# The first group's residual adds in a tiled matmul with bias and residual: from six in a row on GpSimd to four on VectorE, one a tile, and four on GpSimd

## The chip, the cores and the metric

The kernel runs on one core of a Trainium2 chip. The metric is the device time of one execution in microseconds, the median of several runs. A core has five engines with instruction streams of their own: TensorE (PE in the profile; its weight loads are PEld), VectorE (DVE), ScalarE (ACT), GpSimd (POOL) and SyncE (SP), which in this kernel only issues DMAs. Each engine executes its own instructions in order, and semaphores tie the engines together.

## The reference

```python
batch, m, k, n = 16, 512, 1024, 768        # x, weight, bias, residual: float32
def reference(x, weight, bias, residual):
    return (np.matmul(x, weight) + bias + residual).astype(np.float32)
```

Flattened, x is 8192 x 1024, weight 1024 x 768, residual and output 8192 x 768.

## The kernel before

**Tiles and groups.** The 8192 rows are 64 tiles (`n_sub`) of 128 rows. Eight tiles (`G` = 8) form a group, so there are eight groups. A group's x is one load of 4 MB (`load_x`), its residual one load of 3 MB (`load_r`) and its output one store of 3 MB (`store`), but for the first x group, which comes in pieces, and the last store, which goes in pieces. All are issued by SP through one queue, in the order of the program.

**A tile's way.** ScalarE casts the tile's x to bf16 (`cast_x`, L120), three tiles ahead. TensorE transposes it in eight pieces into PSUM (`transpose`, L135, tile `pt`, two buffers). VectorE copies that to SBUF (`copy_xt`, L142, tile `xt`, four buffers). TensorE multiplies it with the weights, which stay in SBUF, in sixteen matmuls (`matmul`, L149, tile `po`, three buffers). VectorE takes the result out of PSUM (`evacuate`).

**What is added where.** For groups 1 to 7 the eviction adds the product to the residual in place (L166), and GpSimd then adds the bias to the same tile, SBUF to SBUF (`add_bias`, L173). Group 0 is different: its residual is not there yet when its tiles are multiplied, so its eviction adds the bias (L163) and writes to a tile of its own, `o_tile`. The residual is added later, SBUF to SBUF, by `add_residual` (L177), eight such adds for the group's eight tiles. Its second argument names the engine; GpSimd is the default.

**The loop** over t (L263 to L286) holds for each tile, in this order: cast of tile t + 3; transposes of tile t + 1, then the matmuls of tile t, on TensorE; copy of tile t + 1 and eviction of tile t on VectorE; and the DMAs that `moves` (L243) lists for this t. The order of each engine's instructions is that of the program, kept by the wrapper `o(...)`. In the kernel before, the residual adds 0 and 1 are on VectorE in tiles 16 and 17, between the copy and the eviction (L277, L278), and 2 to 7 are on GpSimd at the end of tile 15 (L282 to L284), behind the bias add of tile 15 and ahead of that of tile 16.

**Buffers.** Four homes of 3 MB (the ring) hold the residuals and outputs of the groups; `HOME` gives the home of each group: r0 and r3 share home 3, r1 and r4 home 1, r2 and r6 home 0; `o_tile` of group 0 and r5 share home 2. So the load of r3 (listed at t = 17) waits for all eight residual adds, which read r0, that of r4 (t = 21) for the store of group 1, and that of r5 (t = 29) for the store of group 0. Behind the load of r0 and r2 (t = 5), SP's queue goes on with x3 (t = 12), store 1 (t = 15), r3 (t = 17), x4 (t = 20), r4 and store 0 (t = 21), x5 (t = 28), r5 and store 2 (t = 29).

Of the kernel before, what the change touches and what calls it, by code (L numbers as in the profile page):

```python
# [11 lines left out]
G = 8  # L12
# [9 lines left out]
def kernel(  # L22
# [8 lines left out]
    nc = tc.nc  # L31
# [27 lines left out]
    def o(ins):  # L59
        return tc.keep_in_program_order(ins)  # L60
# [49 lines left out]
    def cast_x(t, split=False):  # L110
        if t >= n_sub:
            return
        xb_tiles[t] = slot(xb_pool, "xb", XB_BUFS, [P, K], BF16)
        src = x_tiles[t // G][:, t % G, :]
        if split:
            h = K // 2
            o(nc.scalar.copy(out=xb_tiles[t][:, :h], in_=src[:, :h]))  # L117
            o(nc.vector.tensor_copy(out=xb_tiles[t][:, h:], in_=src[:, h:]))  # L118
        else:
            o(nc.scalar.copy(out=xb_tiles[t], in_=src))  # L120
# [7 lines left out]
    def transpose(t):  # L128
        if t >= n_sub:
            return  # L130
        xb = xb_tiles.pop(t).rearrange("m (h p j) -> m h j p", p=P, j=4)
        pt = slot(pt_pool, "pt", PT_BUFS, [P, n_k, P], BF16)
        for k in range(n_k):
            h, j = divmod(k, 4)
            o(nc.tensor.transpose(out=pt[:, k, :], in_=xb[:, h, j, :], identity=ident))  # L135
        pt_tiles[t] = pt

    def copy_xt(t):
        if t >= n_sub:
            return  # L140
        xt_tiles[t] = slot(xt_pool, "xt", XT_BUFS, [P, n_k, P], BF16)
        o(nc.vector.tensor_copy(out=xt_tiles[t], in_=pt_tiles.pop(t)))  # L142

    def matmul(t, k0=0, k1=n_k):
        if t not in po_tiles:
            po_tiles[t] = slot(po_pool, "po", PO_BUFS, [P, N], FP32)
        for k in range(k0, k1):
            for (n0, nl) in chunks:
                o(nc.tensor.matmul(  # L149
                    po_tiles[t][:, n0:n0 + nl],  # L150
                    lhsT=xt_tiles[t][:, k, :],
                    rhs=w_sb[:, k, n0:n0 + nl],
                    start=(k == 0),
                    stop=(k == n_k - 1),
                ))

    def evacuate(t):


        g, j = divmod(t, G)  # L160
        po = po_tiles.pop(t)
        if g == 0:
            o(nc.vector.tensor_add(out=o_tiles[0][:, j, :], in0=po, in1=bias_bc))  # L163
        else:
            rt = r_tiles[g][:, j, :]
            o(nc.vector.tensor_add(out=rt, in0=po, in1=rt))  # L166
            if t < n_sub - 3:
                add_bias(t)
        xt_tiles.pop(t)

    def add_bias(t, engine=nc.gpsimd):
        rt = r_tiles[t // G][:, t % G, :]
        o(engine.tensor_add(out=rt, in0=rt, in1=bias_bc))  # L173

    def add_residual(t, engine=nc.gpsimd):
        ot = o_tiles[0][:, t, :]
        o(engine.tensor_add(out=ot, in0=ot, in1=r_tiles[0][:, t, :]))  # L177
# [85 lines left out]
    for t in range(3, n_sub - 1):  # L263
        cast_x(t + 3)
        if t == 3:
            matmul(t, 0, 5)
            transpose(t + 1)
            matmul(t, 5, 8)
        elif t == G - 1:
            matmul(t, 0, 2)  # L270
            transpose(t + 1)
            matmul(t, 2, 8)
        else:
            transpose(t + 1)
            matmul(t)
        copy_xt(t + 1)
        if t in (2 * G, 2 * G + 1):  # L277
            add_residual(t - 2 * G, nc.vector)  # L278
        evacuate(t)
        if t in (n_sub - 9, n_sub - 7, n_sub - 5):  # L280
            add_bias(n_sub - 3 + (t - n_sub + 9) // 2)
        if t == 2 * G - 1:  # L282
            for u in range(2, G):
                add_residual(u)  # L284
        for move, *what in moves.get(t, []):
            move(*what)  # L286


    t = n_sub - 1
# [36 lines left out]
```

## Time and profile before

| | us |
|---|---|
| median of 3 runs | 211.21 (211.03 to 211.63) |
| the profiled execution, its time | 210.92 |
| the profiled execution, its span | 209.1 |
| TensorE busy in the span | 199.5 (95%) |
| VectorE busy | 107.3 (51%) |
| ScalarE busy | 67.7 (32%) |
| GpSimd busy | 114.4 (55%) |
| DMA, 87.28 MB | mean 417 GB/s |

The span goes from the first to the last instruction of the profiled execution; its time, as the runs are timed, has 1.8 us more around it. The granted TensorE clock is at full speed throughout. The instructions in question, from the page's groups (count, busy us in total, mean ns of one):

| | engine | count | busy us | mean ns |
|---|---|---|---|---|
| matmuls L149 | TensorE | 978 | 172.1 | 324 |
| copies L142 | VectorE | 64 | 43.6 | 682 |
| evictions L166 | VectorE | 55 | 52.7 | 958 |
| residual adds L177 | VectorE | 2 | 3.3 | 1647 |
| residual adds L177 | GpSimd | 6 | 12.1 | 2056 |
| bias adds L173 | GpSimd | 56 | 101.0 | 1814 |

The matmuls are pipelined, so their durations overlap. Busy shares are averages over the whole span; idle time of an engine that others do not wait for costs nothing.

### The profile page before, as it was taken

How to read it: one execution, taken by the hardware profiler on the slowest of the kernel's cores; microseconds unless marked ns; L12 is line 12 of the kernel's file. 1: busy time of each engine (PE TensorE's matmuls, PEld its weight loads, DVE VectorE, ACT ScalarE, POOL GpSimd, SP SyncE). 2: the span in 40 equal slices, each digit the busy share in tenths (PEclk: the TensorE clock that was granted, in tenths of full speed). 3: DMA queues.
4: the chain of work that ended last, by engine and by line, in shares of the span. 5: the costliest groups of instructions: out<-in, count | busy, mean ns of one | idle time of the engine just before them, and what ended most of it. 6: DMA issues, size and time to landing. Idle time of an engine off the chain costs nothing.

```text
span 209.1 us, 3593 instructions
## 1 busy us (share of the span) xinstructions
PE 199.5 (95%) x1520; PEld 130.8 (63%) x1550; DVE 107.3 (51%) x142; ACT 67.7 (32%) x70; POOL 114.4 (55%) x69
## 2 busy tenths in 40 slices
PE   7679999999999999999999999999999999999992
PEld 2346766666666666666666666666666666666661
DVE  0457555455478545454554554455445445544542
ACT  2446309507331074303632063310733018320000
POOL 2000000365579999966556655655665565599820
PEclk9999999999999999999999999999999999999999
DMA  6999999999999999999999999999999999999994
GB/s 241 416 424 445 461 418 412 464 400 437 431 453 396 418 439 395 454 445 414 431 431 445 418 414 451 434 426 429 417 432 431 461 409 423 417 434 442 409 385 192
DMA packets 5066, 87.28 MB, mean 417 GB/s; under 512 B 565, under 2 KB 694, under 8 KB 1594
## 3 DMA queue, kind: packets, MB, share of 16 engines
q1 hardware_dynamic: 5040, 87.03, 97.8%
q8 instruction: 12, 0.20, 0.4%
q14 instruction: 4, 0.03, 0.0%
q10 hardware_dynamic: 10, 0.01, 0.0%
HBM read 61.88 MB, written 25.17 MB: 416 GB/s over the span
## 4 chain that ended last, share of the span: by engine, by line
PE 82%; DMA 14%; ACT 1%; issue 1%; SPq 0%; DVE 0%; ACTq 0%
PE po L149 69%; PE pt L135 12%; DMA x_tile<-in_x_dram 11%; DMA bias_rows<-in_bias_dram 2%; PE last_ps L293 1%; ACT L76 1%; ACT xb L120 1%; SPq L91 0%; DVE r_tile L296 0%; ACT warm L76 0%; ACTq L120 0%; ACTq L184 0%
## 5 line engine op out<-in xcount | busy, mean ns | idle before, releaser
L149 PE MATMUL po<-w_sb,xt 128*128 128x256 bf16 (+1 forms) x978 | 172.1, 324 | 2.6 <-DVE xt L142 0.8
L173 POOL TENSOR_TENSOR r_tile<-r_tile,bias_bc 128x768 f32<-128x768 f32 x56 | 101.0, 1814 | 85.2 <-DVE r_tile L166 85.2
L149 PEld LDWEIGHTS <-xt 128*128 128x128 bf16 x1008 | 95.8, 98 | 58.9 <-DVE xt L142 1.4
L120 ACT CAST xb<-x_tile 128x1024 bf16<-128x1024 f32 x61 | 61.2, 1044 | 108.5 <-DMA x_tile<-in_x_dram 64.6
L166 DVE TENSOR_TENSOR r_tile<-po,r_tile 128x768 f32<-128x768 f32 x55 | 52.7, 958 | 79.1 <-PE po L149 73.2
L142 DVE COPY xt<-pt 128x1024 bf16<-128x1024 bf16 x64 | 43.6, 682 | 3.1 <-PE pt L135 3.1
L135 PEld LDWEIGHTS <-xb 128*128 128x128 bf16 x512 | 35.4, 113 | 11.0 <-ACT xb L117 3.0
L135 PE MATMUL pt<-ident,xb 128*128 128x128 bf16 x512 | 39.1, 219 | 2.2 <-ACT xb L117 2.2
L177 POOL TENSOR_TENSOR o_tile<-o_tile,r_tile 128x768 f32<-128x768 f32 x6 | 12.1, 2056 | 0.0
L163 DVE TENSOR_TENSOR o_tile<-po,bias_bc 128x768 f32<-128x768 f32 x8 | 7.6, 955 | 7.0 <-PE po L149 7.0
L199 PE MATMUL warm_ps<-warm_in 128*128 128x512 bf16 x14 | 5.3, 530 | 1.0 <-DVE warm L75 1.0
L124 ACT CAST w_sb<-w_stage 128x768 bf16<-128x768 f32 x4 | 3.3, 832 | 3.7 <-DMA w_stage<-in_weight_dram 3.7
L118 DVE CAST xb<-x_tile 128x512 bf16<-128x512 f32 x3 | 1.3, 424 | 6.0 <-DMA x_tile<-in_x_dram 6.0
L199 PEld LDWEIGHTS <-warm_in 128*128 128x128 bf16 x14 | 1.7, 131 | 3.4 <-issue 2.4
L117 ACT CAST xb<-x_tile 128x512 bf16<-128x512 f32 x3 | 1.8, 615 | 5.6 <-DMA x_tile<-in_x_dram 5.6
L177 DVE TENSOR_TENSOR o_tile<-o_tile,r_tile 128x768 f32<-128x768 f32 x2 | 3.3, 1647 | 0.0
L126 DVE CAST w_sb<-w_stage 128x768 bf16<-128x768 f32 x4 | 2.2, 556 | 1.7 <-DMA w_stage<-in_weight_dram 1.7
L293 PE MATMUL last_ps<-w_sb,xt 128*128 128x512 bf16 (+1 forms) x16 | 2.8, 326 | 0.0
L293 PEld LDWEIGHTS <-xt 128*128 128x128 bf16 x16 | 1.6, 98 | 1.1
L296 DVE TENSOR_TENSOR r_tile<-last_ps,r_tile 128x512 f32<-128x512 f32 (+1 forms) x2 | 1.1, 558 | 0.9 <-PE last_ps L293 0.8
L76 ACT ACT_TABLE_LOAD x1 | 1.3, 1283 | 0.7 <-PEq L310 0.7
L227 DVE STREAM_SHUFFLE bias_bc<-bias_rows 128x768 f32<-128x768 f32 x1 | 1.0, 1006 | 0.0
(11 smaller groups left out, 2.1 us busy)
## 6 DMA issues: line engine op xcount, KB each, us to landing
x_tile<-in_x_dram SPq DMA_DIRECT2D x7, 4096.0 KB, 29.2
r_tile<-in_residual_dram SPq DMA_DIRECT2D x8, 3072.0 KB, 17.7
out_dram<-r_tile SPq DMA_DIRECT2D x6, 3072.0 KB, 23.9
x_tile<-in_x_dram SPq DMA_DIRECT2D x4, 1024.0 KB, 8.8
w_stage<-in_weight_dram SPq DMA_DIRECT2D x4, 768.0 KB, 6.5
out_dram<-o_tile SPq DMA_DIRECT2D x1, 3072.0 KB, 31.2
out_dram<-r_tile SPq DMA_DIRECT2D x1, 1536.0 KB
out_dram<-r_tile SPq DMA_DIRECT2D x1, 768.0 KB, 5.5
```

Of the source, the lines that this page charges most:

```text
L76: o(nc.scalar.copy(out=warm, in_=warm))
L120: o(nc.scalar.copy(out=xb_tiles[t], in_=src))
L124: o(nc.scalar.copy(out=w_sb[:, k, :], in_=w_stage[0][:, k, :]))
L135: o(nc.tensor.transpose(out=pt[:, k, :], in_=xb[:, h, j, :], identity=ident))
L142: o(nc.vector.tensor_copy(out=xt_tiles[t], in_=pt_tiles.pop(t)))
L149: o(nc.tensor.matmul(po_tiles[t][:, n0:n0 + nl], lhsT=xt_tiles[t][:, k, :], rhs=w_sb[:, k, n0:n0 + nl], start=(k == 0), stop=(k == n_k - 1),))
L163: o(nc.vector.tensor_add(out=o_tiles[0][:, j, :], in0=po, in1=bias_bc))
L166: o(nc.vector.tensor_add(out=rt, in0=po, in1=rt))
L173: o(engine.tensor_add(out=rt, in0=rt, in1=bias_bc))
L177: o(engine.tensor_add(out=ot, in0=ot, in1=r_tiles[0][:, t, :]))
L199: o(nc.tensor.matmul(warm_ps, lhsT=warm_in, rhs=warm_in[:, None, :].to_broadcast([P, 4, P]), start=True, stop=True))
L293: o(nc.tensor.matmul(ps, lhsT=xt_tiles[t][:, k, :], rhs=w_sb[:, k, n0:n0 + nl], start=(k == 0), stop=(k == n_k - 1)))
```

## The change

VectorE takes four residual adds, 0 to 3, in tiles 14 to 17, each behind the eviction of its tile and not in front of it. GpSimd takes the other four: add 7 in tile 14, between the bias adds of tiles 14 and 15, and 6, 5, 4 at the end of tile 15. VectorE's stream thus gets two adds more (tiles 14 and 15), and in tiles 16 and 17 the order add, eviction becomes eviction, add; GpSimd's loses two. No DMA is added or taken out, and the order of SP's queue is the same.

```diff
         copy_xt(t + 1)
-        if t in (2 * G, 2 * G + 1):
-            add_residual(t - 2 * G, nc.vector)
         evacuate(t)
+        if 2 * G - 2 <= t < 2 * G + 2:
+            add_residual(t - 2 * G + 2, nc.vector)
         if t in (n_sub - 9, n_sub - 7, n_sub - 5):
             add_bias(n_sub - 3 + (t - n_sub + 9) // 2)
-        if t == 2 * G - 1:
-            for u in range(2, G):
+        if t == 2 * G - 2:
+            add_residual(G - 1)
+        elif t == 2 * G - 1:
+            for u in range(G - 2, 3, -1):
                 add_residual(u)
         for move, *what in moves.get(t, []):
             move(*what)
```

## The prediction

> **What bounds the kernel now.** I read the page's chain of waits first, then the waits of TensorE alone, then the timelines of VectorE, GpSimd and TensorE around tiles 14 to 19, and last the busy shares at the very end.
>
> ```profile
> PE 82%; DMA 14%; ACT 1%; issue 1%; SPq 0%; DVE 0%; ACTq 0%
> q1 hardware_dynamic: 5040, 87.03, 97.8%
> ```
>
> The first line is the chain that ended last: 82% of it is TensorE, and the 14% of DMA lies at the start (one piece from 8.09 to 31.50 us, the load of x group 1). From 31.6 us to 205.5 us it names TensorE alone, with 0.05 us of issue every two tiles or so. The second line is the DMA queue, which is almost as full. So two resources run side by side, and the question is which one the end follows.
>
> ```profile
> PE pt L135 <- ACT xb L117: 2.2, 2, 1.1
> PE warm_ps L199 <- DVE warm L75: 1.0, 1, 1.0
> PE po L149 <- DVE xt L142: 0.8, 1, 0.8
> PE po L149 <- ACT w_sb L124: 0.3, 1, 0.3
> ```
>
> These are all the waits of TensorE (us in total, times, longest). By their lines they belong to the start (L117, L75, L124; the 0.8 is at 12.56 us). In the steady loop TensorE never waits, and a tile takes 3.05 us.
>
> ```profile
> 204.00:205.00 1.00, 1.00 (x9) 0.71 (x8) 0.32 (x1) 0.00 (x0) 0.00 (x0) 1.00 0.48 197
> 205.00:206.00 1.00, 0.45 (x5) 0.16 (x2) 0.80 (x2) 0.00 (x0) 0.00 (x0) 1.00 0.83 335
> ```
>
> The last two figures of a row are the DMA share and GB/s. In the last us of matmuls the DMA engines are half idle (0.48): the queue has run dry and the last stores wait for TensorE. So TensorE sets the end: whatever delays it in the loop comes out at the end, and a gain can come only from it.
>
> **The resource that the change touches.** In the timeline of VectorE and GpSimd, the first two figures are start and duration in us.
>
> ```profile
> 60.73 1.81 POOL L173 TENSOR_TENSOR r_tile<-r_tile,bias_bc 128x768 f32<-128x768 f32 x1 [1.24 <-DVE r_tile L166]
> 61.16 2.19 DVE L177 TENSOR_TENSOR o_tile<-o_tile,r_tile 128x768 f32<-128x768 f32 x1
> 62.50 2.53 POOL L177 TENSOR_TENSOR o_tile<-o_tile,r_tile 128x768 f32<-128x768 f32 x1
> 63.28 0.94 DVE L166 TENSOR_TENSOR r_tile<-po,r_tile 128x768 f32<-128x768 f32 x1
> 64.14 0.68 DVE L142 COPY xt<-pt 128x1024 bf16<-128x1024 bf16 x1
> 64.74 1.10 DVE L177 TENSOR_TENSOR o_tile<-o_tile,r_tile 128x768 f32<-128x768 f32 x1
> 65.79 0.96 DVE L166 TENSOR_TENSOR r_tile<-po,r_tile 128x768 f32<-128x768 f32 x1
> ```
>
> The same residual add on VectorE takes 2.19 or 1.10 us, and on GpSimd 2.53 where others take 1.81. The ends explain it. GpSimd's bias add ends at 60.73 + 1.81 = 62.54; VectorE's add, begun at 61.16, ends at 63.35, 0.81 later. GpSimd's next ends at 62.50 + 2.53 = 65.03, 1.68 after VectorE's end. VectorE's second add ends at 65.84, again 0.81 after GpSimd's 65.03. So the two take turns whole instruction by whole instruction: VectorE's add waits for GpSimd's running one to end and then needs 0.81; GpSimd's next then needs 1.68 from there. Evictions (0.96) and copies (0.68) keep their durations, so only the adds with both inputs in SBUF take part.
>
> The cover for a long VectorE add is the slack of the copy behind it, which the timeline of TensorE gives:
>
> ```profile
> 59.49 0.61 PE L135 MATMUL pt<-ident,xb 128*128 128x128 bf16 x8
> 59.94 2.76 PE L149 MATMUL po<-w_sb,xt 128*128 128x512 bf16 x16
> 62.54 0.61 PE L135 MATMUL pt<-ident,xb 128*128 128x128 bf16 x8
> ```
>
> Matmuls of tile 16 start at 59.94, of 17 at 62.99, of 18 at 66.03, of 19 at 69.08, and each needs its copied tile (L142) about 0.05 us before: in the one such wait the copy ended at 11.82 + 0.69 = 12.51 and the matmul began at 12.56.
>
> **The change, step by step.** It takes two adds (1.81 each) off GpSimd, which nobody on the chain waits for, and puts VectorE's adds in tiles 14 to 17, behind the eviction and thus in front of the copy that TensorE needs next. Before, VectorE's two stood in front of the eviction of 16 and 17, whose lateness three PSUM buffers hid. GpSimd's order becomes bias 14, add 7, bias 15, adds 6, 5, 4, bias 16.
>
> An add that meets nobody isn't in the trace. Its bounds are 0.81 (the time after a wait) and 1.10 (the shortest row, wait included); the eviction with as many elements takes 0.96. I take 0.88. An instruction on VectorE starts 0.08 before the one ahead ends, on GpSimd 0.04.
>
> Tile 14: eviction 56.65 to 57.61; add 0 from 57.53 to 58.41; GpSimd's bias add, released by the same eviction at 57.68, finds VectorE first and ends at 58.41 + 1.68 = 60.08 instead of 59.49. Copy 16 ends at 59.01, in time. Tile 15: add 7 on GpSimd from 60.04 to 61.85; VectorE evicts until 60.65 and begins add 1 at 60.57, into it: it ends at 61.85 + 0.81 = 62.67. Copy 17 behind it ends at 63.27, where the matmul was due at 62.99: it begins at 63.33, **0.34 us late**. Tile 16: the eviction ends at 64.15; add 2, begun at 64.07, meets bias 15 (held by add 1, ending 64.35) and ends at 65.16; copy 18 ends at 65.76, due 66.37: in time. Tile 17: add 6, held by add 2, ends at 66.84; add 5 begins at 66.80; VectorE's eviction, late with TensorE, ends at 67.09 and add 3 begins at 67.01, 0.21 too late: it waits for all of add 5 (66.80 + 1.81 = 68.61) and ends at 69.42. Copy 19 ends at 70.02, the matmul begins at 70.08, due at 69.42: **0.66 us late**. From tile 18 on VectorE holds only evictions and copies. Sum: 0.34 + 0.66 = 1.00 us on TensorE, which has no idle time to give back.
>
> With 0.81 for the free add the sum is 0.94, with 0.96 it is 1.08, with 1.10 it is 1.23. If add 0 did not hold GpSimd at all, bias 14 would end at 59.49, add 7 at 61.26, copy 17 would be in time, but add 2 would meet the whole of add 6 and copy 18 would end at 66.94: 0.96 late. Nothing in it shortens a due time, so no bound is below nothing.
>
> Who gets the first turn in tile 14 is not in the trace either. By starts VectorE has it (57.53 against 57.68). If GpSimd had it, add 0 would wait until 59.49 and end at 60.31, copy 16 would end at 60.91 (1.03 late), and a later meeting costs 0.66 again: 1.69.
>
> The Trainium skill's page "SBUF — State Buffer", section "Summary: rules for kernel authors", says of a VectorE instruction with two SBUF inputs beside a GpSimd one that reads SBUF: "the second one to issue **fully blocks** until the first finishes. Schedule whichever is off the critical path". The second sentence speaks against this change, which moves adds from the engine that is off the path to the one that feeds TensorE. By the first, VectorE, which issues earlier in tile 14, goes first there and the sum is 1.00; were the order otherwise it would be 1.69. No row here shows such a near tie.
>
> **Queues.** SP holds, in order, store 1, load r3, load x4, load r4, store 0. Store 1 needs bias 15, now 64.35 instead of 62.54: 1.8 us later, but it lies behind x3, whose landing let the cast go at 73.33, so it costs nothing while 8.9 us remain. Load r3 needs all eight adds: 71.1 instead of 74.65; x4 behind it comes as much earlier. Both lie behind store 1, and load r4 waits for its landing (issued at 80.60) as before. Add 0 needs r0, which by the list of DMA issues was issued at 23.55 and landed 32.3 later, at 55.85, 1.7 us before its new start; were it later than that, copies and TensorE would queue behind it.
>
> **The end.** The last store is issued 0.03 us after the last add and lands 2.4 us later. The rows of 204 to 206 allow little hiding, at most 0.1 to 0.2 us of the 1.00; I take 0.95. The profiled execution has a span of 209.1 and a time of 210.92, so 210.1 and 211.9 after; it lies 0.29 under the median of 211.21, and so the median becomes about 212.1.
>
> **Rivals.** First, GpSimd goes first in tile 14: 211.21 + 1.7 = 212.9. For it: the difference is 0.15 us of recorded starts. Against it: VectorE's add is next in its queue and needs no signal from another engine. Second, only one collision: if add 3 asks before add 5 begins (0.21 us), it waits for nothing, copy 19 is in time, and 0.34 remains: 211.5; likewise if the turns are looser than two meetings show. Third, on the other side: the transfers, not TensorE, set the time. The DMA share dips to 0.91 and 0.93 from 70 to 80 us, around the load r3 at 74.65; 10 us at 8% are 0.8 us, and r3 comes 3.5 us earlier. If that dip were r3's lateness and the stream set the end, the time would be 210.4. It decides from the point where TensorE waits for a load anywhere after 32 us; no such wait is in its list, and the queue is half idle at 204, so it would need both to be misread.
>
> **How the numbers follow.** Forecast (0.9 to 1.2 us lost) 0.62; GpSimd first 0.14; one collision or none 0.18; transfers 0.06. A measurement here tells about 0.3%, 0.63 us, from no change. Slower by more than that: forecast, the first rival and a little of the second, 0.78. Within it: most of the second and a sliver of the third, 0.17. Faster: 0.05. The predicted time is 212.1. The range runs from the second rival's 211.5 to the first's 212.9; for the free add's bounds and some hiding at the end I set 211.4 to 212.9.
>
> **What would show it.** In the profile after: TensorE waiting for L142 twice, some 0.34 and 0.66 us, at tiles 17 and 19 (about 63 and 70 us), and none elsewhere after 33 us; four VectorE adds of about 0.9, 2.1, 1.1 and 2.4 us; bias 14 at 2.4 instead of 1.81; load r3 near 71; the last store about 1 us later. I am wrong if the copies of 17 and 19 end in time, if TensorE's waits vanish at the end, or if the wait moves to tile 16.

## The result and the profile after

| | before | after |
|---|---|---|
| median of 22 runs, us | 211.20 (210.77 to 212.32) | 211.61 (211.33 to 212.93) |
| ratio, 95% interval | | 1.0027 (1.0015 to 1.004) |
| the profiled execution, its time and span, us | 210.92, 209.1 | 211.50, 209.7 |
| last store issued, landed, us | 205.94, 208.3 | 207.00, 208.85 |

The change makes the kernel slower by 0.57 us by the ratio (0.32 to 0.85; the medians differ by 0.41), where 0.95 had been forecast. The high end of the runs after goes with a lower clock: in 7 of the 22 the mean granted clock was 0.991 to 0.992 and the time 212.6 to 212.9, in the other 15 it was 211.3 to 211.9 at 0.998 or more; the last section shows one execution of that kind.

The chain of waits of the kernel after, by engine, and its DMA queue:

```profile
PE 79%; DMA 14%; DVE 3%; issue 1%; ACT 1%; SPq 0%; ACTq 0%
q1 hardware_dynamic: 5040, 87.03, 97.5%
```

VectorE, with 0% before, now has 3% of the chain; the rest is as it was. TensorE's waits after 33 us, from the list of waits of the kernel after (us in total, times, longest; the kernel before has none there):

```profile
PE po L149 <- DVE xt L142: 0.7, 2, 0.5
```

Two waits for a copied tile, as forecast. Where they are, the timeline of TensorE after shows:

```profile
59.92 2.76 PE L149 MATMUL po<-w_sb,xt 128*128 128x512 bf16 x16
62.52 0.61 PE L135 MATMUL pt<-ident,xb 128*128 128x128 bf16 x8
63.37 2.77 PE L149 MATMUL po<-w_sb,xt 128*128 128x512 bf16 x16 [0.24 <-DVE xt L142]
65.98 0.61 PE L135 MATMUL pt<-ident,xb 128*128 128x128 bf16 x8
66.43 2.76 PE L149 MATMUL po<-w_sb,xt 128*128 128x512 bf16 x16
69.03 0.61 PE L135 MATMUL pt<-ident,xb 128*128 128x128 bf16 x8
70.13 2.77 PE L149 MATMUL po<-w_sb,xt 128*128 128x512 bf16 x16 [0.49 <-DVE xt L142]
```

At 3.05 us a tile, the matmuls of tile 17 were due at 59.92 + 3.05 = 62.97 and those of tile 19 at 66.43 + 3.05 = 69.48. They begin 0.40 and 0.65 us late. The bracket gives less (0.24, 0.49), because it counts from the modelled end of the transposes, which overlap the next matmul. What made the copies late, in the timelines of VectorE and GpSimd after:

```profile
57.50 0.95 DVE L177 TENSOR_TENSOR o_tile<-o_tile,r_tile 128x768 f32<-128x768 f32 x1
60.54 2.17 DVE L177 TENSOR_TENSOR o_tile<-o_tile,r_tile 128x768 f32<-128x768 f32 x1
62.64 0.68 DVE L142 COPY xt<-pt 128x1024 bf16<-128x1024 bf16 x1
64.14 1.06 DVE L177 TENSOR_TENSOR o_tile<-o_tile,r_tile 128x768 f32<-128x768 f32 x1
67.06 2.42 DVE L177 TENSOR_TENSOR o_tile<-o_tile,r_tile 128x768 f32<-128x768 f32 x1
69.40 0.68 DVE L142 COPY xt<-pt 128x1024 bf16<-128x1024 bf16 x1
```

```profile
57.66 2.46 POOL L173 TENSOR_TENSOR r_tile<-r_tile,bias_bc 128x768 f32<-128x768 f32 x1 [1.25 <-DVE r_tile L166]
60.09 1.81 POOL L177 TENSOR_TENSOR o_tile<-o_tile,r_tile 128x768 f32<-128x768 f32 x1
61.86 2.54 POOL L173 TENSOR_TENSOR r_tile<-r_tile,bias_bc 128x768 f32<-128x768 f32 x1
64.36 6.79 POOL L177 TENSOR_TENSOR o_tile<-o_tile,r_tile 128x768 f32<-128x768 f32 x3
```

VectorE's four adds take 0.95, 2.17, 1.06 and 2.42 us. GpSimd's add 7 runs from 60.09 to 61.90, VectorE's add 1 asks at 60.54, gets its turn at 61.90 and ends at 62.71, 0.81 later; the copy of tile 17 stands behind it. Add 3 asks at 67.06; the second of GpSimd's three adds in the last row, add 5, began 0.22 us before, at 66.84 by the trace.

So TensorE is 1.06 us late, and the last store is issued 1.06 us later. But it lands only 0.55 us later. The other half went at the very end. The list of DMA issues has the last store's time from issue to landing, first of the kernel before, then of the kernel after:

```profile
out_dram<-r_tile SPq DMA_DIRECT2D x1, 128.0 KB, 2.4
```

```profile
out_dram<-r_tile SPq DMA_DIRECT2D x1, 128.0 KB, 1.8
```

Each of the 16 DMA engines reports its share of a transfer when it has landed. For the last store these reports in the trace are:

```
          first   median   last engine (us)
before    207.6    207.7    208.3
after     208.7    208.8    208.8
```

Before, a few engines were 0.6 us behind the others: the last store, ready at 205.94, still waited for their backlog. After, all engines had caught up and the store needed 1.85 us for itself.

### The profile page after: what moved, and what is told of

Its sections match the earlier page's. It is cut to its first block, busy times and chain, and to the rows that moved or that the text cites. A ratio compares the mean times of both kernels' runs of the same rounds, so it can differ in the third digit from the quotient of the medians.

```text
span 209.7 us, 3623 instructions
## 1 busy us (share of the span) xinstructions
PE 201.2 (96%) x1550; PEld 130.8 (62%) x1550; DVE 110.4 (53%) x144; ACT 68.1 (32%) x70; POOL 112.2 (53%) x67
## 4 chain that ended last, share of the span: by engine, by line
PE 79%; DMA 14%; DVE 3%; issue 1%; ACT 1%; SPq 0%; ACTq 0%
PE po L149 67%; DMA x_tile<-in_x_dram 11%; PE pt L135 11%; DMA w_stage<-in_weight_dram 3%; DVE o_tile L177 2%; PE last_ps L295 1%; DVE xt L142 1%; ACT xb L120 1%; SPq L91 0%; DVE r_tile L298 0%; DVE r_tile L166 0%; ACTq L120 0%
## 5 line engine op out<-in xcount | busy, mean ns | idle before, releaser
L149 PE MATMUL po<-w_sb,xt 128*128 128x512 bf16 x1008 | 174.2, 326 | 1.9 <-DVE xt L142 1.5
L173 POOL TENSOR_TENSOR r_tile<-r_tile,bias_bc 128x768 f32<-128x768 f32 x56 | 102.3, 1835 | 88.4 <-DVE r_tile L166 88.4
L177 POOL TENSOR_TENSOR o_tile<-o_tile,r_tile 128x768 f32<-128x768 f32 x4 | 8.6, 2174 | 0.0
L177 DVE TENSOR_TENSOR o_tile<-o_tile,r_tile 128x768 f32<-128x768 f32 x4 | 6.6, 1649 | 0.0
```

The costliest lines, as they stand in the source:

```text
L149: o(nc.tensor.matmul(po_tiles[t][:, n0:n0 + nl], lhsT=xt_tiles[t][:, k, :], rhs=w_sb[:, k, n0:n0 + nl], start=(k == 0), stop=(k == n_k - 1),))
```

## The experiments

The theory is that of two ends. The time is the later of (a) TensorE's last store plus its own 1.85 us and (b) the end of the DMA stream on its slowest engines. The collisions delay (a) by 1.06 us; the kernel before ends on (b), at 208.3, about half a us later than its (a) at 205.94 + 1.85 = 207.79. Each experiment's runs are compared with runs of the kernel before on the same chip.

**A pure delay of TensorE.** To the kernel before, five, ten or two matmuls are added in tile 19; the tile's own first matmul overwrites what they write.

```diff
             transpose(t + 1)
+            if t == 19:
+                filler(t, 5)
             matmul(t)
...
+    def filler(t, n):
+        po_tiles[t] = slot(po_pool, "po", PO_BUFS, [P, N], FP32)
+        for i in range(n):
+            o(nc.tensor.matmul(po_tiles[t][:, 0:512], lhsT=xt_tiles[t][:, 0, :],
+                               rhs=w_sb[:, 0, 0:512], start=True, stop=True))
```

> The kernel before with five more matmuls of 512 columns in tile 19, whose result the tile's own first matmul overwrites: a pure delay of TensorE of 5 x 0.214 = 1.07 us, the same as the change caused, with VectorE and GpSimd untouched. Theory (the kernel before ends on the slowest DMA engines' backlog, some 0.5 us after what TensorE's end alone would allow, so that the first 0.5 us of a delay are hidden): last store issued 1.07 us later, time 0.5 to 0.6 us longer, ratio 1.0025. Rival (the delay comes out whole, and the change gained 0.5 us elsewhere by the earlier load of r3): ratio 1.005.

> As the one with five, with ten more matmuls: 2.14 us. Theory of a fixed cushion of 0.5 us: time 1.6 us longer, ratio 1.0076. Rival (a half of any delay is hidden): 1.1 us, ratio 1.005. Rival (nothing is hidden): 2.1 us, ratio 1.010.

> The kernel before with two more matmuls in tile 19, 0.43 us of delay on TensorE alone. Theory of the two ends: hidden, ratio within 0.1% of 1. Rival (delays come out whole, or by half): 1.002 or 1.001.

| | delay of TensorE | last store issued | landed after | ratio to before | median, us |
|---|---|---|---|---|---|
| two | 0.43 | 206.37 | 2.4 | 0.9993 (0.9969 to 1.0016) | 211.41 |
| five | 1.07 | 207.01 | 1.9 | 1.0004 (0.9989 to 1.0018) | 211.52 |
| ten | 2.14 | 208.06 | 1.9 | 1.0049 (1.003 to 1.0068) | 212.64 |

From five to ten the time grows by 1.12 us for 1.07 us of delay, so there all of it comes out; up to five almost nothing does. That is a fixed cushion, not a share: the 1.0049 of ten is by itself what the rival of one half forecast, but half of the delay of five would give 1.0025, which lies outside the interval of five. The row of two matmuls decides nothing by itself, since its interval holds 1.001 as well as 1. The size of the cushion was underestimated, and the 1.0025 and 1.0076 expected of five and ten missed with it: on the chip on which five and ten ran the kernel before took 211.6 (27 runs), so ten cost 1.04 us and about 1.1 were hidden, where 0.5 had been expected. With five the time is 211.52, what the changed kernel takes, with r3 loaded as late as in the kernel before: where TensorE's end is the later one, the earlier r3 of the change buys no time.

**The kernels before and after once more, on one chip.** No edit.

> The kernel before once more, for a trace on the same chip as the three that follow. Theory (time is the later of two ends: TensorE's last store plus its own 1.85 us, and the DMA stream's, which is set by the slowest of the 16 DMA engines): the last store is issued at 205.9 to 206.1 us and lands 2.3 us or more after, with some engines 0.5 us or more behind the others, so the stream's end is the later one. Rival (TensorE's end is the later one): the last store lands within 1.9 us, all 16 engines within 0.2 us.

> The changed kernel once more. Theory of the two ends: the last store is issued 1.06 us later than in the kernel before and lands 1.85 us after that, all engines within 0.2 us of each other; most runs lie at 211.5, whatever the kernel before does on this chip, and a run above 212.3 is one in which the stream lost more than a us. Rival (the change costs a fixed 0.3%): on a chip where the kernel before takes 211.6, the changed one takes 212.2.

Before: 211.6 (10 runs), ratio 1.0002 (0.9988 to 1.0017) to 21 more runs of the same kernel; its last store is issued at 205.94, lands on its first engine at 207.6 and on its last at 208.6. After: 211.65, ratio 1.0011 (0.9998 to 1.0024) to the 211.54 of those 21 runs, a loss that is not clear of the noise there; its last store is issued at 207.08 and lands from 208.8 to 209.0. In its two sets of runs the changed kernel took 211.61 and 211.65, while the kernel before moved from 211.20 to 211.54. A fixed cost of 0.3% would have given 212.1 on this chip.

**The adds in front of the eviction.** The changed kernel, with its four VectorE adds moved ahead.

```diff
-        evacuate(t)
         if 2 * G - 2 <= t < 2 * G + 2:
             add_residual(t - 2 * G + 2, nc.vector)
+        evacuate(t)
```

> The changed kernel with VectorE's four adds put in front of the eviction of their tile again, GpSimd's order as in the change. Theory (only the copy that feeds TensorE is short of slack; a late eviction is hidden by the three PSUM buffers): VectorE's adds still meet GpSimd's and take up to 2.5 us, but no copy is late, TensorE loses nothing and the time is that of the kernel before, within 0.1%. Rival (the collisions themselves cost, wherever the adds stand): TensorE loses some 0.5 to 1 us and the ratio stays near 1.0027.

Ratio 0.9992 (0.9978 to 1.0005). VectorE's add 1 still takes 2.19 us, but TensorE waits for no copy after 33 us and the last store is issued at 206.08. The collisions as such cost TensorE nothing; it is the copy behind them that does. It is the trace that shows this: on this chip the delay of 1.07 us by five matmuls did not show in the time either, so the time cannot tell the theory from its rival. r3 is loaded as early as in the change (71.19), without a gain that is clear of the noise.

**GpSimd's adds moved back.** The changed kernel, with GpSimd's four residual adds behind the bias add of tile 17.

```diff
-        if t == 2 * G - 2:
-            add_residual(G - 1)
-        elif t == 2 * G - 1:
-            for u in range(G - 2, 3, -1):
+        if t == 2 * G + 1:
+            for u in range(G - 1, 3, -1):
                 add_residual(u)
```

> The changed kernel with GpSimd's four residual adds all moved behind the bias add of tile 17, so that VectorE's four adds in tiles 14 to 17 meet only bias adds, each of which is released by the eviction just ahead of VectorE's add and so comes second. Theory (two collisions with GpSimd's residual adds delay the copies of tiles 17 and 19, and TensorE by 0.41 + 0.66 us): every VectorE add takes 0.95 us, TensorE waits for no copy after 33 us, the last store is issued within 0.1 us of the kernel before (205.9), and the time is that of the kernel before, within 0.1%. Rival (the adds cost by their mere place behind the eviction, whoever GpSimd serves): TensorE still loses about 1 us and the time stays at 1.0027 of before.

The half of the expectation that speaks of TensorE held, the other missed. The list of line L177 for this kernel (duration min/median/max in ns):

```profile
L177 DVE TENSOR_TENSOR o_tile<-o_tile,r_tile x4: 948/949/949, 57.6 to 66.7; 128x768 f32<-128x768 f32 x4
```

No collision, no wait of TensorE, the last store issued at 205.97. Yet the time is 212.5, ratio 1.0046 (1.0029 to 1.0062), and the last store lands 3.7 us after its issue:

```profile
out_dram<-r_tile SPq DMA_DIRECT2D x1, 128.0 KB, 3.7
```

The stream had become about a us longer. What differs for it is SP's queue. Its timeline, of this kernel:

```profile
63.25 0.35 SPq L105 DMA_DIRECT2D out_dram<-r_tile  x1
76.46 0.33 SPq L101 DMA_DIRECT2D r_tile<-in_residual_dram  x1
76.88 0.38 SPq L91 DMA_DIRECT2D x_tile<-in_x_dram  x1
```

r3, which waits for the last residual add, goes out at 76.46, not at 74.65, and x4 behind it. That raised the question whether a late r3 alone does it.

**All eight adds on GpSimd; all eight on VectorE.** The first is the kernel before without its two VectorE adds (`for u in range(G)` at the end of tile 15). The second is the changed kernel with the condition `2 * G - 2 <= t < 3 * G - 2` and no GpSimd adds.

> The kernel before with all eight residual adds on GpSimd, behind the bias add of tile 15. TensorE loses nothing; the load of r3 is issued at about 77.1 us instead of 74.65, as late as in the variant with GpSimd's adds moved back (76.5), which took a us more without any loss on TensorE. Theory (that us came from the late issue of r3, which leaves DMA engines short of work): the time is about 212.5 and the DMA stream ends a us later. Rival (it came from something else in that variant, VectorE's four adds or GpSimd's later order): the time is that of the kernel before.

> All eight residual adds on VectorE, one in each of tiles 14 to 21, behind the eviction; none on GpSimd. They meet only bias adds that come second, so TensorE loses nothing; the load of r3 is issued at about 79.9 us, when the fastest DMA engines have been through with the store before it for a us. Theory (a late r3 costs the DMA stream): the stream ends 1 to 2 us later, time 212.5 to 213.5. Rival (r3 has room until the store before it has landed on all engines at 80.5): the time is that of the kernel before.

| | r3 issued | last store issued, landed | ratio to before |
|---|---|---|---|
| after | 71.17 | 207.00, 208.85 | 1.0027 |
| adds in front | 71.19 | 206.08, 208.76 | 0.9992 |
| before | 74.65 | 205.94, 208.3 | 1 |
| GpSimd's adds moved back | 76.46 | 205.97, 209.7 | 1.0046 |
| all on GpSimd | 76.75 | 205.93, 209.8 | 1.0045 (1.0031 to 1.0059) |
| all on VectorE | 80.03 | 208.39, 212.4 | 1.0164 (1.0148 to 1.0179) |

The stream became longer in both, as the theory of the late r3 says, though all on VectorE cost more than expected and TensorE did lose there: it waited 2.1 us, since r3 landed only at 91.1 and the eviction of tile 24 needs it. In all three x4, behind r3 in the queue, went out late as well; the runs do not separate the two loads. So the kernel before has about 1.8 us to spare at most before r3 is too late, although the store ahead of r3 lands only at 80.6. In all on VectorE the queue ran dry ahead of r3: nothing was moved (0.00 MB) from 80.30 to 80.92. In the other two the windows of 100 to 105 us show most of the loss, first of the kernel before, then of GpSimd's adds moved back, then of all on GpSimd (the last two figures are DMA share and GB/s):

```profile
100.00:105.00 5.00, 4.95 (x37) 3.20 (x36) 2.41 (x4) 2.56 (x3) 3.43 (x2) 1.00 0.97 411
```

```profile
100.00:105.00 5.00, 4.95 (x37) 3.20 (x37) 2.44 (x4) 2.83 (x3) 3.39 (x2) 1.00 0.99 362
```

```profile
100.00:105.00 5.00, 4.95 (x37) 3.20 (x36) 2.41 (x4) 2.91 (x3) 3.43 (x2) 1.00 1.02 367
```

The engines are as busy and move 11 to 12% less. This is not at r3 itself, which lands only 0.2 to 0.3 us late, but at r4, issued at 80.6 to 80.9 in all three, which lands at 104.8, 106.2 and 106.3. Why a late r3 slows that transfer stays open; it wasn't tried further.

**One collision less.** The changed kernel with add 7 at the end of tile 15, ahead of 6, 5 and 4.

```diff
-        if t == 2 * G - 2:
-            add_residual(G - 1)
-        elif t == 2 * G - 1:
-            for u in range(G - 2, 3, -1):
+        if t == 2 * G - 1:
+            for u in range(G - 1, 3, -1):
                 add_residual(u)
```

> The changed kernel with GpSimd's add 7 moved from tile 14 to the end of tile 15, ahead of 6, 5 and 4: VectorE's adds of tiles 14 and 15 meet no residual add of GpSimd's. Theory: the collision of tile 17 goes, VectorE's add 2 meets one and copy 18 is late by about 0.4 us, the only wait for a copy after 33 us; the last store is issued 0.4 us later than in the kernel before, which is less than what its DMA stream hides, so the time is that of the kernel before within 0.1%. Rival (a delay of TensorE comes out whole, the hiding seen with 1.06 us being something else): 0.2% longer.

Ratio 0.999 (0.9965 to 1.0015). One wait for a copy, in front of tile 18: its matmuls begin at 67.51 where 64.06 + 3.05 = 67.11 was due, 0.40 late. The last store of the profiled execution was issued not 0.4 but 1.49 us later than in the kernel before, because the granted clock fell to one half for a while (below). The interval is too wide to tell 0% from 0.1%, but the rival's 0.2% lies outside.

**All the traces together.** In the twelve profiled executions, the kernels before and after and the ten of this section, the time is 2.6 to 2.7 us more than the moment at which the last store has landed on its last engine. In five of them (after, after once more, five, ten, add 7 later) that store lands 1.85 to 1.89 us after its issue, on all engines within 0.21 us of each other. In the other seven it takes 2.36 to 4.03 us and the engines lie 0.7 to 2.4 us apart. These are the two ends.

No version was faster than the kernel before; the best, the adds in front, equals it.

## Why the prediction was right or wrong

**What bounds the kernel.** Wrong in its last step. That "TensorE sets the end" was read from a DMA share of 0.48 between 204 and 205 us. The share is a mean over 16 engines: of the store issued at 200.94, the first engine had landed its part at 204.0 and the last only at 206.4. So some were through, and a few had work until 208. The delay experiments show that the kernel before ends on these. The chain of waits could not show it either: it is followed back from the last instruction, which ends at 205.91, and the landing of the last store at 208.3 is no part of it.

**The turns of the two engines.** Right. The rule taken from two meetings (0.81 after GpSimd's end, 1.68 after VectorE's) gave all four durations of VectorE's adds to 0.1 us, with 0.95 for the add that meets nobody where 0.88 had been taken. VectorE went first in tile 14 (57.50 against 57.66, and GpSimd's bias add took 2.46 us), so the first rival fell; that the one which issues first goes first is what the Trainium skill's page "SBUF — State Buffer", section "Who interferes with whom", says, and this near tie agrees. Both collisions came, so the second fell.

**TensorE's loss.** Forecast 0.34 + 0.66 = 1.00 us, measured 0.40 + 0.65, and 1.06 at the last store. That nothing downstream gives it back until the end was right too.

**Queues.** Store 1 at 64.42, r3 at 71.17, r4 at 80.56: as forecast, and free of cost. That an earlier r3 gains nothing was right: with the adds in front, TensorE loses nothing, r3 comes 3.5 us earlier, and the time stays within the noise. The third rival was half right. The transfers do set the end of the kernel before, though TensorE never waits for a load after 32 us and the queue looks half idle at 204; neither sign, by which the rival was set aside, speaks of the slowest engines. Its gain did not come, and the dip in the DMA share from 70 to 80 us was not r3's lateness: in the kernel after it is still there (0.91 and 0.94). What the prediction did not see is that r3 was near an edge on its other side.

**The end.** This is the term that was mis-sized: "at most 0.1 to 0.2 us of the 1.00" was to be hidden, and 0.51 of 1.06 was, in the profiled pair; on another chip about 1.1 of a TensorE delay of 2.14. The profiled execution took 211.50 where 211.9 had been worked out, and the median 211.61 where 212.1 stood. The direction held, and the mechanism did up to the last store's issue. But at 0.27% the loss lies just under the bound of 0.3%, on the side to which the chances gave 0.17. And that it showed so clearly is in part luck: on the chip where the kernel before takes 211.54, the ratio is 1.0011.

**Slips without consequence.** 0.95 on 211.21 makes 212.16, not 212.1. In the case that add 0 does not hold GpSimd, the prediction's own turns let add 2 ask at 63.62, before bias 15 ends at 62.07 + 1.68 = 63.75; copy 18 is then in time, and copy 19 about 0.4 us late, in place of 0.96 us at tile 18. From 31.6 us the chain first names ScalarE's cast, and TensorE alone from 32.7.

## What to carry to other kernels

When two resources are both nearly full, ask for each where its own end lies, and look at the last transfer engine by engine: a mean DMA share of one half can be a few late engines that still set the end, and then the first part of any delay elsewhere is free. An add that is moved to the idle-looking engine must be costed with what stands behind it: the same collision costs nothing in front of an eviction with three PSUM buffers and 0.4 to 0.65 us in front of the copy that feeds TensorE. A load that lands on time may still have been issued near its edge; delaying its issue, and that of the load behind it, by 1.8 us cost more than the collisions did.

## What was not expected of the hardware

In some runs of most kernels the mean granted clock was 0.991 to 0.993. One such execution was profiled (add 7 at the end of tile 15); its windows near the start show a fall of the clock (the figure before the DMA share is the granted clock):

```profile
12.00:13.00 1.00, 0.76 (x3) 0.37 (x4) 0.65 (x2) 0.83 (x1) 0.00 (x0) 0.76 1.04 436
13.00:14.00 1.00, 1.00 (x5) 0.54 (x4) 0.09 (x1) 0.09 (x1) 0.00 (x0) 0.50 1.07 442
14.00:15.00 1.00, 1.00 (x5) 0.39 (x4) 1.00 (x3) 0.74 (x1) 0.00 (x0) 0.50 1.00 414
```

The clock is at one half for 3.4 us, from 12.52 on. TensorE is 1.07 us behind the kernel before from tile 9 on (its transposes begin at 36.19 against 35.12): by chance the size of the change's own loss. In the 3.4 us ahead of the fall TensorE's matmuls were busy for 1.75 us, with no gap over 0.9 us; why the clock falls in some executions and not in others stays open. That the other runs with such a mean clock lost it in the same way is likely, but they have no trace. If so, they are a further test of the two ends. Of the runs of the kernel before that stood beside the experiments, 57 with a mean clock of 0.9955 or more have a median of 211.40 and 19 below 0.994 have 211.71, 0.3 more. In the 22 runs of the kernel after, 15 have 211.52 and 7 have 212.75, 1.2 more. That fits: the same loss of clock is mostly hidden in the one and comes out whole in the other, whose cushion the collisions had used up.
